# Staging S5 scan inputs in DRAM, running the scan ahead of three gate projections, and mid-chunk states on 128 lanes

## The chip, the cores and the metric

The kernel runs on one core of a Trainium2 chip. The metric is the device time of one execution in microseconds (us); the kernel before stands at a median of 2649.24 us over 3 runs (2646.02 to 2655.04). Engines are named as in the profile: PE is TensorE's matmul, PEld its weight load, DVE is VectorE, ACT is ScalarE, POOL is GpSimd, SP is SyncE, which issues most of the transfers.

## The reference

The kernel computes one step of a two-layer trunk for a prompt of 2048 positions and 8 samples of 4 positions, width 1024. Layer A is a chunked gMLP, which the change does not touch. Layer B is an S5 state-space mixer:

```python
xb, z = jnp.split(h @ w_in, 2, axis=-1)
xg = xb.astype(jnp.float32).reshape(bn, seq_len, N_GROUPS_B, SSM_GROUP)
bu_re = jnp.einsum('blgk,gpk->blgp', xg, bbr)
bu_im = jnp.einsum('blgk,gpk->blgp', xg, bbi)
acr, aci, hr, hi = lax.associative_scan(_combine, (ar, ai, bu_re, bu_im), axis=1)
y = jnp.einsum('gkp,blgp->blgk', cr, hr) - jnp.einsum('gkp,blgp->blgk', ci, hi)
y = y.reshape(bn, seq_len, EXP_B) + d_skip.astype(jnp.float32) * xb.astype(jnp.float32)
y = jax.nn.gelu(y).astype(h.dtype)
y = (y @ w_glu1 + b_glu1) * jax.nn.sigmoid(y @ w_glu2 + b_glu2)
out = (y * jax.nn.silu(z)) @ w_out
```

There are 64 groups of 16 channels, each with a complex state of 64 numbers. `xb` feeds the states; `z` is the gate, which is first needed in the gated unit after the states' output `y`.

## The kernel before, in words

The 2048 positions are cut into 128 chunks of 16, and each chunk into two halves of 8. `layer_b` runs in this order: the gate projection of position block 0 (`z_phase`, L817), the `xb` projections of blocks 0 and 1 (`xb_step`, L798), the gate projection of block 1, then the `xb` projections of blocks 2 and 3 mixed with eight calls of `state_in` (L838), the `scan` (L878), the gate projections of blocks 2 and 3, and the states' output `s5_out` (L889). `layer_c` (L966) then reads y back and runs the gated unit `glu` and the output projection.

A projection of a block is 8 weights of 24 PE matmuls (128x512) each: fp32 operands are split into two fp32r parts by ACT (`whi`, L68) and DVE (`wlo`, L69) and multiplied three times. Block 3, which also carries the samples, goes as halves of 256 and 288 columns, 48 matmuls per weight. In the profile these read `mm<-hn`. Each weight is a 512 KB load on SP's queue into `wst`, a pool of two buffers that is free again once DVE has made `wlo`. The gate z goes to DRAM (`zd`) from ACT's queue.

`state_in(u)` makes, for four groups per lane half (128 lanes), the chunk halves' state inputs: the first half's go to `G1` (L857), a tile of 128x2x32x128 fp32 (32 KB a partition) that stays in SBUF, the second half's to `S`. Sixteen DVE scalar_tensor_tensor of 128x128 (L862) add the decayed first half, and `advance` (L866) with steps 1, 2 and 4 combines chunks into spans of 8 chunks. `scan` runs over the 16 spans, serially, on DVE.

`s5_out` runs 16 units u, two (gh = 0, 1: the two lane halves) for each group set of four groups. For a pair of units there are

- loads on SP: T, Xo (two), Co for each unit,
- once a pair (gh = 0): `advance` down the tree with steps 4, 2, 1 (12 DVE tensor_tensor), and on POOL two times `gt` (L911) and `G` (L912), 128x512 each, which turn G1 into (first half's input + imaginary part of the decayed state),
- for each unit: ACT copies the chunk-start states into H (L917, 64x512), and eight DVE scalar_tensor_tensor of 64x128 (L919) write the mid-chunk states into H's second part,
- for each unit: four pairs of fp32 matmuls with 264 columns, `aux<-Xo,T` and `aux<-H,Co` (each shows as two records), the GELU on ACT (L927, `Y`), and stores of Y to DRAM (`yd`, `ysd`) on SP.

Which engine runs what when is set by the framework's scheduler from priorities. `p0` (L783) notes the priority before the last gate projection, and `s5_out`, written after it, is placed at that priority: its instructions and the gate projections written after `p0` are interleaved, s5_out first where it is ready. Before the change only block 3's gate projection stands behind `p0`. `load_y` (L987) reads y back (`yst<-yd`), ACT and DVE split it (L68, L69), and `mm<-y` is the first work of layer C.

Of the kernel before, what the change touches and what calls it, by code (L numbers as in the profile page):

```python
# [8 lines left out]
F32 = mybir.dt.float32  # L9
# [5 lines left out]
MUL, ADD, SUB = ALU.mult, ALU.add, ALU.subtract  # L15
# [3 lines left out]
NB = 4  # L19
# [3 lines left out]
AL = 512  # L23
TXP = 640
L = 16
NC_ = 128
G = 64
K16 = 16
CW = NC_ + 8
# [5 lines left out]
class Trunk:  # L35
# [701 lines left out]
    def layer_b(self, s0):  # L737
        with ExitStack() as sr:
            zp = s0.enter_context(self.pool("zp", 2))
            with ExitStack() as s1:  # L740
                hb3 = s1.enter_context(self.pool("hb3"))
                with ExitStack() as s2:
                    hb2 = s2.enter_context(self.pool("hb2"))
                    with ExitStack() as s3:
                        hb1 = s3.enter_context(self.pool("hb1"))
                        hbs = {1: hb1, 2: hb2, 3: hb3}
                        c2 = s3.enter_context(self.pool("c2"))
                        xf = s3.enter_context(self.pool("xf"))
                        self.xp = s3.enter_context(self.pool("xp2", 4))
                        g1 = self.load_gpre(c2, 1)  # L750
                        gens = [self.prep_block(b, self.x1c(b), self.x1s, g1, hbs[b], f"hb{b}")
                                for b in range(1, NB)]
                        self.hn1 += [next(g) for g in gens]
                        steps = (x for g in gens for x in g)
                        for fb in range(8):
                            self.z_phase(zp, [0], [fb])
                            if fb < 3:
                                next(steps)
                        for fb in range(8):
# [5 lines left out]
                    self.nc.vector.memset(S[:, :, :, 0], 0.0)  # L765
                    G1 = sr.enter_context(self.pool("gp", side="right")).tile([128, 2, 32, NC_], F32, name="G1")
                    with ExitStack() as s3:
                        xf = s3.enter_context(self.pool("xf2"))
                        sp = s3.enter_context(self.pool("sp", 2))
                        for i in range(4):  # L770
                            for gh in range(2):
                                self.xb_step(xf, i + 4 * gh, [2, 3])
                                if i:
                                    self.state_in(sp, S, G1, 2 * (i - 1) + gh)
                        for gh in range(2):
                            self.state_in(sp, S, G1, 6 + gh)
                        t1 = sp.tile([128, 2, 2, 4, 64], F32, tag="adv", name="sc", bufs=1)[:, :, :, 0, 0:32]
                        self.scan(S, t1)
                    opa = sr.enter_context(self.pool("opa", 3, side="right"))
                    self.z_phase(zp, [2])  # L780
                opb = sr.enter_context(self.pool("opb", 2, side="right"))
                fp = sr.enter_context(self.pool("fp", side="right"))
                p0 = self.tc.cur_priority  # L783
                self.z_phase(zp, [3])
            self.yq = s0.enter_context(self.pool("yq"))
            self.yp = s0.enter_context(self.pool("yp", 2))
            with self.tc.high_priority(offset=self.tc.cur_priority - p0):
                self.s5_out(fp, opa, opb, S, G1)
            self.y0 = self.load_y(0)

    def relay(self, dst, o, c0, n):
# [43 lines left out]
        for h in range(2):  # L835
            self.nc.sync.dma_start(X[:, :, h], s[h][:, g0:g0 + ng, :])

    def state_in(self, sp, S, G1, u):  # L838
# [19 lines left out]
        for g in range(gl, gl + 4):  # L858
            for r in range(2):
                for i in range(2):  # L860
                    x = S[:, r, g, 1:1 + NC_]
# [27 lines left out]
    def s5_out(self, fp, opa, opb, S, G1):  # L889
        nc, I = self.nc, self.I  # L890
        stt = nc.vector.scalar_tensor_tensor
        h0 = fp.tile([128, 64, 8], F32, name="h0")
        nc.sync.dma_start(h0, I["h0k"])
        for u in range(16):
            gl, gh, gu = (u // 2) * 4, u % 2, ((u // 2) % 2) * 4
            fb = u // 4 + 4 * gh
# [31 lines left out]
            d = self.yd[fb].rearrange("(h j) k g c -> h (j k) g c", h=2)  # L928
# [166 lines left out]
    def build(self):  # L1095
        tc = self.tc
        with self.ctx as s:
# [9 lines left out]
            t = lambda n, shape: dr.tile(shape, F32, name=n)  # L1107
# [4 lines left out]
            self.bind = [t(f"bind{i}", [128, 8, 128]) for i in range(8)]  # L1112
            self.xd = [t(f"xd{i}", [16, 16, 8, CW]) for i in range(8)]
            self.zd = [t(f"zd{i}", [128, NB, 16, 32]) for i in range(8)]
            self.zsd = [t(f"zsd{i}", [128, NS]) for i in range(8)]
            self.yd = [t(f"yd{i}", [16, 16, 8, NC_]) for i in range(8)]
            self.ysd = [t(f"ysd{i}", [4, 16, 8, 8]) for i in range(8)]
# [97 lines left out]
```

## Time and profile before

| | us |
|---|---|
| median of 3 runs | 2649.24 |
| the profiled execution's own time | 2648.36 |
| its span, first to last instruction | 2646.6 |
| PE busy over the span | 2577.8 (97%) |
| DVE, ACT, POOL busy | 1519.2 (57%), 906.4 (34%), 470.8 (18%) |
| s5_out's stretch, first `aux<-Xo,T` to last `aux<-H,Co` | about 1963.4 to 2088.4 |

All times are of one profiled execution; 1.8 us of its time lie outside the span. PE is close to fully busy over the whole program, so what is to be read are the stretches in which it is not. PE records of matmuls in a row overlap, so a mean duration is more than the distance from one to the next; the prices of matmuls are taken from unbroken chains of them. The granted clock column (PEclk) is 1.00 when TensorE is granted 2.4 GHz and 0.50 when it is granted 1.2 GHz.

### The profile page before, as it was taken

Reading aid. Unit: us, or ns where it says so; the run is one execution under the profiler, and the core shown is the slowest. Engines: PE = TensorE matmul, PEld = TensorE weight load, DVE = VectorE, ACT = ScalarE, POOL = GpSimd, SP = SyncE. Lnnn points to the kernel's source line nnn. Section 1 sums busy time; section 2 is a strip of 40 time slices with the busy share of each in tenths; the row PEclk is TensorE's granted clock in tenths of the full one; section 3 lists DMA queues with packets and bytes.
Section 4 is the critical chain, followed back from the end, with each engine's and each line's share of the span. In section 5 each row is a group of like instructions: output and inputs, shape, how many; then the busy total and the mean of one; then the engine's idle time right before and its main releaser. Section 6 shows DMA issues by size and latency. Waiting matters only on the chain.

```text
span 2646.6 us, 34651 instructions
## 1 busy us (share of the span) xinstructions
PE 2577.8 (97%) x13163; PEld 2192.5 (83%) x13163; DVE 1519.2 (57%) x2805; ACT 906.4 (34%) x1488; POOL 470.8 (18%) x644
## 2 busy tenths in 40 slices
PE   9999999999999999999999999999997899999998
PEld 7888877888878888887999877889986688888896
DVE  5974577743575633563733448314899746464645
ACT  3333343322333222432322334324644433333331
POOL 1454475100120000000000120000013212121220
PEclk9999999999999999999999999999998999999999
DMA  4253345422575222242322336445668735454542
GB/s 160 90 165 110 115 119 176 138 88 91 156 207 193 93 88 95 90 153 92 118 80 80 104 106 208 108 137 157 197 218 242 213 119 168 150 170 149 165 129 100
DMA packets 234839, 366.66 MB, mean 139 GB/s; under 512 B 64512, under 2 KB 154880, under 8 KB 234672
## 3 DMA queue, kind: packets, MB, share of 16 engines
q1 hardware_dynamic: 181344, 307.17, 36.7%
q0 software_dynamic: 13344, 36.63, 4.6%
q10 hardware_dynamic: 39984, 20.65, 2.9%
q8 instruction: 103, 1.69, 0.3%
q14 instruction: 64, 0.52, 0.1%
HBM read 307.45 MB, written 56.92 MB: 138 GB/s over the span
## 4 chain that ended last, share of the span: by engine, by line
PE 81%; DVE 10%; DMA 4%; issue 3%; POOL 1%; ACT 1%; SPq 1%; DVEq 0%; POOLq 0%; ACTq 0%
PE mm L59 79%; DVE wlo L69 1%; PE aux L59 1%; DVE H L919 1%; PE aux L137 1%; DVE adv L874 1%; DVE S L876 1%; DMA td<-vt 1%; DVE adv L873 1%; DMA x<-x1d 0%; DMA x<-in_xp_dram 0%; DVE adv L875 0%; POOL co L687 0%; DMA bind<-bo 0%; POOL ct L687 0%
## 5 line engine op out<-in xcount | busy, mean ns | idle before, releaser
L59 PE MATMUL mm<-hn,whi 128*128 128x512 f32 (+2 forms) x3840 | 1016.6, 353 | 3.4 <-ACT a L334 3.4
L69 DVE TENSOR_TENSOR wlo<-wst,whi 128x1024 fp32r<-128x1024 f32 x396 | 504.7, 1275 | 551.8 <-ACT whi L68 540.5
L59 PEld LDWEIGHTS mm<-hn,whi 128*128 128x128 f32 x3840 | 674.5, 189 | 92.1 <-ACT a L334 3.6
L68 ACT CAST whi<-wst 128x1024 fp32r<-128x1024 f32 x400 | 419.5, 1049 | 939.0 <-PE mm L59 811.3
L59 PE MATMUL mm<-hn,wlo 128*128 128x512 f32 (+2 forms) x1920 | 676.0, 352 | 3.7 <-DVE wlo L69 3.7
L59 PEld LDWEIGHTS mm<-hn,wlo 128*128 128x128 f32 x1920 | 362.7, 189 | 50.3 <-DVE wlo L69 4.5
L59 PE MATMUL mm<-whi,gs 128*128 128x512 f32 x1024 | 334.5, 399 | 10.6 <-ACT gs L68 5.1
L59 PE MATMUL mm<-y,whi 128*128 128x512 f32 (+2 forms) x1280 | 336.1, 351 | 3.4 <-ACT y L68 3.0
L59 PE MATMUL mm<-whi,hn 128*128 128x512 f32 x1024 | 325.7, 394 | 0.5 <-ACT hn L68 0.5
L59 PEld LDWEIGHTS mm<-y,whi 128*128 128x128 f32 x1280 | 224.2, 188 | 37.9 <-ACT y L68 3.8
L59 PEld LDWEIGHTS mm<-whi,gs 128*128 128x128 f32 x1024 | 194.6, 191 | 56.3 <-ACT gs L68 7.6
L59 PEld LDWEIGHTS mm<-whi,hn 128*128 128x128 f32 x1024 | 193.3, 189 | 43.8 <-ACT hn L68 0.7
L59 PE MATMUL mm<-y,wlo 128*128 128x512 f32 (+2 forms) x640 | 224.4, 351 | 0.0
L59 PE MATMUL mm<-wlo,hn 128*128 128x512 f32 x512 | 201.5, 393 | 3.6 <-DVE wlo L69 3.5
L59 PE MATMUL mm<-wlo,gs 128*128 128x512 f32 x512 | 202.2, 395 | 0.0
L59 PE MATMUL mm<-whi,m 128*128 128x512 f32 x512 | 159.8, 390 | 0.0
L69 DVE TENSOR_TENSOR gs<-gq,gs 128x512 fp32r<-128x512 f32 (+1 forms) x128 | 92.5, 723 | 108.9 <-ACT gs L68 108.6
L348 DVE SCALAR_TENSOR_TENSOR gq<-mm,lng,Rp 128x512 f32<-128x512 f32 x64 | 48.0, 750 | 173.2 <-PE mm L59 173.2
L68 ACT CAST gs<-gq 128x512 fp32r<-128x512 f32 (+1 forms) x128 | 80.2, 628 | 177.8 <-PE mm L59 168.7
L59 PEld LDWEIGHTS mm<-y,wlo 128*128 128x128 f32 x640 | 120.3, 188 | 16.2
L59 PEld LDWEIGHTS mm<-wlo,hn 128*128 128x128 f32 x512 | 96.9, 189 | 25.7 <-DVE wlo L69 4.6
L59 PEld LDWEIGHTS mm<-wlo,gs 128*128 128x128 f32 x512 | 97.5, 190 | 19.9
(291 smaller groups left out, 2684.8 us busy)
## 6 DMA issues: line engine op xcount, KB each, us to landing
wst<-in_wuz_dram SPq DMA_DIRECT2D x128, 512.0 KB, 3.4
wst<-in_wv_dram SPq DMA_DIRECT2D x64, 512.0 KB, 3.5
wst<-in_woa_dram SPq DMA_DIRECT2D x64, 512.0 KB, 3.3
wst<-in_wg_dram SPq DMA_DIRECT2D x64, 512.0 KB, 3.6
wst<-in_wib_dram SPq DMA_DIRECT2D x48, 512.0 KB, 4.2
wst<-in_wob_dram SPq DMA_DIRECT2D x32, 512.0 KB, 3.6
Xi<-xd SPq DMA_DIRECT2D x32, 272.0 KB, 4.2
Xo<-xd SPq DMA_DIRECT2D x32, 272.0 KB, 5.4
```

Of the source, the lines that this page charges most:

```text
L59: self.nc.tensor.matmul(out, lhsT, rhs, start=start, stop=stop)
L68: self.nc.scalar.copy(hi, src)
L69: (e or self.nc.vector).tensor_tensor(lo, src, hi.bitcast(F32), SUB)
L137: nc.tensor.transpose(b[:, k * 128:k * 128 + P], x[:, o:o + 128], self.ident[:P, :P])
L348: nc.vector.scalar_tensor_tensor(g3, s3, self.lng[:, db:db + 1], R, MUL, ADD)
L873: v.tensor_tensor(t[:, 0], d[0], S[:, :, g, src], MUL)
L874: v.tensor_tensor(t[:, 1], d[1], S[:, ::-1, g, src], MUL)
L876: v.tensor_tensor(S[:, :, g, dst], t[:, 0], S[:, :, g, dst], ADD)
L919: stt(H[q, g, CW:], S[p, r, gl + g, 0:NC_], self.d8[p, 0, r, gl + g:gl + g + 1], G1[p, r, gl + g], MUL, ADD)
```

## The change

- The gate projection of block 1 moves from ahead of the `xb` projections of blocks 2 and 3 to behind the scan, and `p0` is taken before it. So the gate projections of blocks 1, 2 and 3 all stand at the priority that lets `s5_out` interleave with them.
- `G1` is gone. `state_in(u)` fills a small tile `G` (128x2x4x128) and stores it to a DRAM tensor `gd[u]` (512 KB, ACT's queue). `s5_out` loads it back once a pair (`Go`, 512 KB, SP's queue, two buffers).
- POOL's 32 tensor_tensor (`gt`, `G`) and the 128 DVE scalar_tensor_tensor of 64x128 are replaced by 128 DVE scalar_tensor_tensor of 128x128 on `Go` (16 a pair, real and imaginary part), and 32 ACT copies of 64x512 put the result into H.
- The pool `opa` has 2 buffers by default in place of 3; T and Xo keep their own 4, so this meets Co (3 to 2) and the new Go.

```diff
@@ layer_b
-                        for fb in range(8):
-                            self.xb_step(xf, fb, [0, 1])
-                            if fb % 2 == 0:
-                                next(steps, None)
                         self.z_phase(zp, [1])
-                    S = self.hnp.tile([128, 32, 2, CW + 1], F32, tag="hn", name="S", align_bytes=AL).rearrange("p g r c -> p r g c")
-                    G1 = sr.enter_context(self.pool("gp", side="right")).tile([128, 2, 32, NC_], F32, name="G1")
...
+                            for fb in range(8):
+                                self.xb_step(xf, fb, [0, 1])
+                                if fb % 2 == 0:
+                                    next(steps, None)
+                            for _ in steps:
+                                pass
...
+                            for gh in range(2):
+                                self.state_in(sp, S, 6 + gh)
+                            t1 = sp.tile([128, 2, 2, 4, 64], F32, tag="adv", name="sc", bufs=1)[:, :, :, 0, 0:32]
+                            self.scan(S, t1)
+                        p0 = self.tc.cur_priority
                         self.z_phase(zp, [1])
-                    opa = sr.enter_context(self.pool("opa", 3, side="right"))
+                    opb = sr.enter_context(self.pool("opb", 2, side="right"))
+                    opa = sr.enter_context(self.pool("opa", 2, side="right"))
+                    fp = sr.enter_context(self.pool("fp", side="right"))
                     self.z_phase(zp, [2])
-                opb = sr.enter_context(self.pool("opb", 2, side="right"))
-                fp = sr.enter_context(self.pool("fp", side="right"))
-                p0 = self.tc.cur_priority
                 self.z_phase(zp, [3])
@@ state_in
+        G = sp.tile([128, 2, 4, NC_], F32, tag="G", name="G")
...
-                        nc.scalar.copy(S[p, r, g, 1:1 + CW] if h else G1[p, r, g], o[r * 64:r * 64 + 64])
+                        nc.scalar.copy(S[p, r, g, 1:1 + CW] if h else G[p, r, 2 * e:2 * e + 2], o[r * 64:r * 64 + 64])
+        nc.scalar.dma_start(self.gd[u], G)
...
-                    nc.vector.scalar_tensor_tensor(x, G1[:, r ^ i, g], self.d8[:, i, r, g:g + 1], x, MUL, ADD)
+                    x = S[:, r, gl + g, 1:1 + NC_]
+                    nc.vector.scalar_tensor_tensor(x, G[:, r ^ i, g], self.d8[:, i, r, gl + g:gl + g + 1], x, MUL, ADD)
@@ s5_out
             if gh == 0:
+                G = opa.tile([128, 2, 4, NC_], F32, tag="G", name="Go")
+                nc.sync.dma_start(G, self.gd[u // 2])
                 for i in (4, 2, 1):
                     self.advance(opb, S, gl, i, slice(0, NC_, 2 * i), slice(i, NC_, 2 * i))
-                gs = slice(gl, gl + 4)
-                for r in range(2):
-                    t = opb.tile([128, 4, NC_], F32, tag="gt", name="gt", bufs=1)
-                    d = self.d8[:, 1, r, gs].rearrange("p (g o) -> p g o", o=1).to_broadcast([128, 4, NC_])
-                    nc.gpsimd.tensor_tensor(t, d, S[:, 1 - r, gs, 0:NC_], MUL)
-                    nc.gpsimd.tensor_tensor(G1[:, r, gs], G1[:, r, gs], t, ADD)
+                for g in range(4):
+                    for r in range(2):
+                        for i in range(2):
+                            stt(G[:, r, g], S[:, r ^ i, gl + g, 0:NC_], self.d8[:, i, r, gl + g:gl + g + 1],
+                                G[:, r, g], MUL, ADD)
...
-                for g in range(4):
-                    stt(H[q, g, CW:], S[p, r, gl + g, 0:NC_], self.d8[p, 0, r, gl + g:gl + g + 1], G1[p, r, gl + g],
-                        MUL, ADD)
+                nc.scalar.copy(H[q, :, CW:], G[p, r])
```

The order that the scheduler makes of it shows at three places. The first is PE's order at the end of s5_out, up to the first matmul of layer C. Before the change (`mm<-y` is layer C):

```order
L59 MATMUL aux<-Xo,T 128x264 x3
L59 MATMUL aux<-H,Co 128x264
L59 MATMUL aux<-Xo,T 128x264
L59 MATMUL aux<-H,Co 128x264 x3
L59 MATMUL aux<-Xo,T 128x264 x2
L59 MATMUL aux<-H,Co 128x264
L59 MATMUL aux<-Xo,T 128x264 x2
L59 MATMUL aux<-H,Co 128x264 x3
L953 MATMUL aux<-ident,hp 64x128
L960 MATMUL aux<-ident,hs 128x128 x4
L59 MATMUL mm<-y,whi 128x512 x2
```

and with it:

```order
L59 MATMUL aux<-Xo,T 128x264
L59 MATMUL aux<-H,Co 128x264
L59 MATMUL mm<-hn,whi 128x288 x2
L59 MATMUL mm<-hn,wlo 128x288
L59 MATMUL mm<-hn,whi 128x256 x2
L59 MATMUL mm<-hn,wlo 128x256
L59 MATMUL mm<-hn,whi 128x288 x2
L59 MATMUL mm<-hn,wlo 128x288
L957 MATMUL aux<-ident,hp 64x128
L59 MATMUL mm<-hn,whi 128x256
L964 MATMUL aux<-ident,hs 128x128 x4
L59 MATMUL mm<-hn,whi 128x256
```

Before, the last units of s5_out stand back to back and layer C follows at once; the 253 halves of block 3's gate that the order has behind the first `aux<-Xo,T` are spread over the units before. Now 116 matmuls of 512 columns and 211 halves stand between the first `aux<-Xo,T` and the last `aux<-H,Co`, and 173 halves more between that and the first `mm<-y`. Ahead of the first `state_in` matmul, 192 matmuls of 512 columns (block 1's gate) are gone; between the last one and the first `aux<-Xo,T` stand 182 of 512 columns, where there were 108 of them and 131 halves.

The second place is DVE's order over one pair of units in the middle of s5_out. Before:

```order
L873 TENSOR_TENSOR adv<-d_72,S 128x8x16
L874 TENSOR_TENSOR adv<-d_72,S 128x8x16
L875 TENSOR_TENSOR adv<-adv 128x8x16
L876 TENSOR_TENSOR S<-adv,S 128x2x4x16
L873 TENSOR_TENSOR adv<-d_71,S 128x8x32
L874 TENSOR_TENSOR adv<-d_71,S 128x8x32
L875 TENSOR_TENSOR adv<-adv 128x8x32
L919 SCALAR_TENSOR_TENSOR H<-S,d_69,G_14456 64x128 x4
L876 TENSOR_TENSOR S<-adv,S 128x2x4x32
L873 TENSOR_TENSOR adv<-d_70,S 128x512
L874 TENSOR_TENSOR adv<-d_70,S 128x512
L919 SCALAR_TENSOR_TENSOR H<-S,d_69,G_14456 64x128 x4
```

and with the change:

```order
L878 TENSOR_TENSOR adv<-d_71,S 128x8x32
L879 TENSOR_TENSOR adv<-d_71,S 128x8x32
L880 TENSOR_TENSOR adv<-adv 128x8x32
L881 TENSOR_TENSOR S<-adv,S 128x2x4x32
L878 TENSOR_TENSOR adv<-d_70,S 128x512
L879 TENSOR_TENSOR adv<-d_70,S 128x512
L880 TENSOR_TENSOR adv<-adv 128x512
L881 TENSOR_TENSOR S<-adv,S 128x2x4x64
L917 SCALAR_TENSOR_TENSOR Go<-S,d_69,Go 128x128 x9
L878 TENSOR_TENSOR adv<-d_72,S 128x8x16
L917 SCALAR_TENSOR_TENSOR Go<-S,d_69,Go 128x128
L879 TENSOR_TENSOR adv<-d_72,S 128x8x16
```

The count for a pair is the same, 12 tensor_tensor and 16 scalar_tensor_tensor; the latter now write `Go`, which must have been loaded, where they wrote H from G1.

The third place is SP's queue in the middle of s5_out, with the change:

```order
L839 DMA Xo<-xd_102 128x4x136 x2
L81 DMA wst<-in_wib_dram 128x1024
L911 DMA Go<-gd_119 128x1024
L908 DMA Co<-cod_77 128x512
L934 DMA yd_133<-Y 128x4x128 x2
L935 DMA ysd_141<-Y 64x4x8
L81 DMA wst<-in_wib_dram 128x1024 x2
L904 DMA T<-td_90 128x512
L908 DMA Co<-cod_81 128x512
```

Here the loads of the gate's weights (`wst`) and of `Go` stand between the loads and stores of the units; before, the stretch had two weight loads of the gate, six of layer C, and no `Go`.

## Rows read from the trace of the kernel before

**Rows 1.** Windows: us, busy PE, PEld, DVE, ACT, POOL, PEclk, DMA share, GB/s.

```profile
1963.40:2088.40 125.00, 102.31 (x513) 88.37 (x514) 122.05 (x231) 58.35 (x126) 46.53 (x47) 0.89 0.85 250
2088.40:2098.40 10.00, 6.61 (x29) 4.58 (x27) 2.75 (x6) 4.51 (x8) 3.91 (x4) 1.00 0.95 271
```

**Rows 2.** PE's waits from 1815 to 2100: waiter and releaser, total, times, longest.

```profile
PE aux L59 <- DVE H L919: 14.8, 6, 4.0
PE aux L59 <- POOL gt L911: 5.5, 1, 5.5
PE mm L59 <- ACT y L68: 3.0, 2, 2.0
...
PE aux L59 <- DMA Xo<-xd: 1.5, 1, 1.5
PE mm L59 <- DVE y L69: 0.4, 1, 0.4
```

**Rows 3.** PE's groups by line in 1963.4 to 2088.4.

```profile
L59 PE MATMUL aux<-H,Co 128*128 128x264 f32 x128 | 44.4, 455 | 22.7 <-DVE H L919 14.8 <-POOL gt L911 5.5 <-issue 2.3
L59 PE MATMUL mm<-hn,whi 128*128 128x256 f32 (+1 forms) x168 | 40.6, 329 | 0.0
L59 PE MATMUL aux<-Xo,T 128*128 128x264 f32 x128 | 40.0, 407 | 1.5 <-DMA Xo<-xd 1.5
L59 PE MATMUL mm<-hn,wlo 128*128 128x288 f32 x85 | 28.4, 334 | 0.0
```

**Rows 4.** The chain from 1640 to 1960: start us, us, what.

```profile
1703.83 21.78 PE mm L59 x96
1726.21 89.02 PE mm L59 x456
```

**Rows 5.** PE's timeline at the end of s5_out: start us, us, what.

```profile
2085.66 1.05 PE L59 MATMUL aux<-Xo,T 128*128 128x264 f32 x4
2086.55 1.50 PE L59 MATMUL aux<-H,Co 128*128 128x264 f32 x6
```

**Rows 6.** DVE's groups by line in 1963.4 to 2088.4.

```profile
L919 DVE SCALAR_TENSOR_TENSOR H<-S,d,G 64x128 f32<-64x128 f32 x128 | 40.4, 375 | 0.7
L874 DVE TENSOR_TENSOR adv<-d,S 128x128 f32<-128x128 f32 (+2 forms) x21 | 22.5, 1074 | 0.0
```

**Rows 7.** DVE's groups by line in 1815 to 1935, where `state_in` runs.

```profile
L862 DVE SCALAR_TENSOR_TENSOR S<-G,d,S 128x128 f32<-128x128 f32 x128 | 35.0, 355 | 21.6 <-ACT S L857 21.6
...
L69 DVE TENSOR_TENSOR wlo<-wst,whi 128x1024 fp32r<-128x1024 f32 x11 | 13.4, 1222 | 10.5 <-ACT whi L68 10.4
L874 DVE TENSOR_TENSOR adv<-d,S 128x512 f32<-128x512 f32 (+2 forms) x23 | 13.3, 578 | 0.0
```

**Rows 8.** Windows, DVE alone: us, busy (instructions), PEclk, DMA share, GB/s.

```profile
1815.00:1935.00 120.00, 94.95 (x231) 1.00 0.61 185
```

**Rows 9.** Transfers in 1963.4 to 2088.4: total, and issues with median landing.

```profile
DMA packets 45764, 31.31 MB, mean 250 GB/s; under 512 B 6567, under 2 KB 40172, under 8 KB 45755
...
wst<-in_wg_dram SPq DMA_DIRECT2D x6, 512.0 KB, 3.7
zd<-z ACTq DMA_DIRECT2D x6, 256.0 KB, 4.7
yst<-yd SPq DMA_DIRECT2D x6, 256.0 KB, 4.9
wst<-in_wib_dram SPq DMA_DIRECT2D x2, 512.0 KB, 5.1
```

**Rows 10.** Windows of 10 us whose DMA share is over 1.

```profile
1960.00:1970.00 10.00, 8.49 (x62) 8.02 (x61) 9.79 (x13) 4.31 (x8) 5.64 (x5) 1.00 1.06 335
1970.00:1980.00 10.00, 7.69 (x45) 6.81 (x44) 9.79 (x24) 3.98 (x8) 1.44 (x2) 1.00 1.07 340
...
2010.00:2020.00 10.00, 6.36 (x37) 5.55 (x35) 9.76 (x16) 4.20 (x9) 5.43 (x5) 0.96 1.08 322
...
2040.00:2050.00 10.00, 6.75 (x40) 5.90 (x38) 9.79 (x15) 5.50 (x12) 6.15 (x6) 0.99 1.09 325
...
2070.00:2080.00 10.00, 4.85 (x10) 3.37 (x11) 9.82 (x19) 3.11 (x7) 4.98 (x5) 0.69 1.08 301
```

**Rows 11.** SP's waits in 1963.4 to 2098.4.

```profile
SPq L81 <- DVE wlo L69: 23.8, 5, 6.4
```

**Rows 12.** ACT's groups by line in 1963.4 to 2088.4.

```profile
L917 ACT COPY H<-S 64x512 f32<-64x512 f32 x32 | 19.9, 620 | 16.1 <-DVE S L876 10.0 <-DVE adv L874 5.7
```

More of the change, by code (lines that the diff above doesn't have):

```diff
@@ L745, in layer_b @@
                         hb1 = s3.enter_context(self.pool("hb1"))
[L746 to L752, printed above, removed]
@@ L753, in layer_b @@
-                        self.hn1 += [next(g) for g in gens]
-                        steps = (x for g in gens for x in g)
-                        for fb in range(8):
[L756 to L759, printed above, removed]
-                            self.xb_step(xf, fb, [0, 1])
-                            if fb % 2 == 0:
-                                next(steps, None)
@@ L763, in layer_b @@
-                        self.z_phase(zp, [1])
-                    S = self.hnp.tile([128, 32, 2, CW + 1], F32, tag="hn", name="S", align_bytes=AL).rearrange("p g r c -> p r g c")
-                    self.nc.vector.memset(S[:, :, :, 0], 0.0)
-                    G1 = sr.enter_context(self.pool("gp", side="right")).tile([128, 2, 32, NC_], F32, name="G1")
[L767 to L778, printed above, removed]
@@ L779, in layer_b @@
-                    opa = sr.enter_context(self.pool("opa", 3, side="right"))
+                        with ExitStack() as s4:
+                            hbs = {1: hb1, 2: hb2, 3: hb3}
+                            c2 = s4.enter_context(self.pool("c2"))
+                            xf = s4.enter_context(self.pool("xf"))
+                            self.xp = s4.enter_context(self.pool("xp2", 4))
+                            g1 = self.load_gpre(c2, 1)
+                            gens = [self.prep_block(b, self.x1c(b), self.x1s, g1, hbs[b], f"hb{b}")
+                                    for b in range(1, NB)]
+                            self.hn1 += [next(g) for g in gens]
+                            steps = (x for g in gens for x in g)
+                            for fb in range(8):
+                                self.z_phase(zp, [0], [fb])
+                                if fb < 3:
+                                    next(steps)
+                            for fb in range(8):
+                                self.xb_step(xf, fb, [0, 1])
[3 more added lines that the diff above has]
+                                pass
@@ new lines, in layer_b @@
+                        S = self.hnp.tile([128, 32, 2, CW + 1], F32, tag="hn", name="S",
+                                          align_bytes=AL).rearrange("p g r c -> p r g c")
+                        self.nc.vector.memset(S[:, :, :, 0], 0.0)
+                        with ExitStack() as s4:
+                            xf = s4.enter_context(self.pool("xf2"))
+                            sp = s4.enter_context(self.pool("sp", 2))
+                            for i in range(4):
+                                for gh in range(2):
+                                    self.xb_step(xf, i + 4 * gh, [2, 3])
+                                    if i:
+                                        self.state_in(sp, S, 2 * (i - 1) + gh)
+                            for gh in range(2):
+                                self.state_in(sp, S, 6 + gh)
+                            t1 = sp.tile([128, 2, 2, 4, 64], F32, tag="adv", name="sc", bufs=1)[:, :, :, 0, 0:32]
+                            self.scan(S, t1)
@@ L787, in layer_b @@
             with self.tc.high_priority(offset=self.tc.cur_priority - p0):
-                self.s5_out(fp, opa, opb, S, G1)
+                self.s5_out(fp, opa, opb, S)
             self.y0 = self.load_y(0)
@@ L836, in load_x, with state_in @@
             self.nc.sync.dma_start(X[:, :, h], s[h][:, g0:g0 + ng, :])
-    def state_in(self, sp, S, G1, u):
+    def state_in(self, sp, S, u):
         nc = self.nc
+        G = sp.tile([128, 2, 4, NC_], F32, tag="G", name="G")
         gl, g0 = 4 * u, (u % 2) * 4
@@ L887, in scan, with s5_out @@
             v.tensor_tensor(S[:, :, :, c], t1, t2, ADD)
-    def s5_out(self, fp, opa, opb, S, G1):
+    def s5_out(self, fp, opa, opb, S):
         nc, I = self.nc, self.I
@@ L904, in s5_out @@
             if gh == 0:
+                G = opa.tile([128, 2, 4, NC_], F32, tag="G", name="Go")
+                nc.sync.dma_start(G, self.gd[u // 2])
                 for i in (4, 2, 1):
                     self.advance(opb, S, gl, i, slice(0, NC_, 2 * i), slice(i, NC_, 2 * i))
-                gs = slice(gl, gl + 4)
-                for r in range(2):
-                    t = opb.tile([128, 4, NC_], F32, tag="gt", name="gt", bufs=1)
-                    d = self.d8[:, 1, r, gs].rearrange("p (g o) -> p g o", o=1).to_broadcast([128, 4, NC_])
-                    nc.gpsimd.tensor_tensor(t, d, S[:, 1 - r, gs, 0:NC_], MUL)
-                    nc.gpsimd.tensor_tensor(G1[:, r, gs], G1[:, r, gs], t, ADD)
+                for g in range(4):
+                    for r in range(2):
+                        for i in range(2):
+                            stt(G[:, r, g], S[:, r ^ i, gl + g, 0:NC_], self.d8[:, i, r, gl + g:gl + g + 1],
+                                G[:, r, g], MUL, ADD)
             H = opb.tile([128, 4, CW + NC_], F32, tag="H", name="H")
@@ L1114, in build @@
             self.zd = [t(f"zd{i}", [128, NB, 16, 32]) for i in range(8)]
+            self.gd = [t(f"gd{i}", [128, 2, 4, NC_]) for i in range(8)]
             self.zsd = [t(f"zsd{i}", [128, NS]) for i in range(8)]
```

2 lines of the change are left out of this document (removed).

## The prediction

> **What bounds the kernel now.** The page's first part comes first: PE is busy 97% of the span, so a change to work beside PE gains nothing unless it removes a stretch in which PE stands or runs slowly. The windows by stage show the only long one near this change, s5_out and the ten microseconds behind it [rows 1]: PE is busy 102.31 of 125.00 us at a mean granted clock of 0.89 of 2.4 GHz, then 6.61 of 10.00. DVE is busy 122.05 of the 125.00, so DVE sets the pace there. The waits say the same [rows 2]: PE stands on DVE's H (14.8 us) and once on POOL's gt (5.5), then on the first y (3.0 and 0.4). The list starts at 1815 and has no wait of PE before the 1.5 us ahead of the first Xo,T: state_in and the scan are covered by gate projections.
>
> How much can be won? I price PE's work at full clock. A 512-column matmul is 21.78/96 = 0.2269 us [rows 4]. The chain of 456 is 312 of these and 144 halves by the program's order: (89.02 - 70.8)/144 = 0.1266 for a half. Four records of 264 columns lie between the starts 2085.66 and 2086.55 [rows 5], 0.2225 each. The stage has 256 such records and 253 halves [rows 3]: 57.0 + 32.0, with 0.6 for transposes 89.6 of 125 us. The next 10 us hold 25 matmuls of layer C (29 records less 4 transposes), 5.7 us. So 95.3 of 135 us are work and **39.7 us are lost**: 22.7 + 3.4 us of standing [rows 1], and the remaining 13.6 us at the lower clock, 1.2 GHz, which agrees with 0.11 x 125 from the clock column.
>
> **The change, part by part.** *The move.* Behind the first Xo,T there are now 116 matmuls of 512 columns and 211 + 173 halves in place of 253 halves: 26.3 + 131 x 0.1266 = 42.9 us more work. It is missing ahead of it, so the first Xo,T comes at 1963.4 - 42.9 = 1920.5, if the stretch before stays unbroken. The scan's cover is as long as before: 182 x 0.2269 = 41.3 us against 108 x 0.2269 + 131 x 0.1266 = 41.1. The 1.5 us ahead of the first Xo,T stays in both. Let S be the new time from first Xo,T to the end of s5_out. Behind it come 173 halves (21.9 us), a wait for y, and the 25 matmuls (5.7). Layer C's first chain now has 21.9 us of cover; that could hide all 3.4 us of today's waits, or none, as y's eight tiles come one by one through two buffers. I keep the 3.4. The point that was 2098.4 is then 1920.5 + S + 21.9 + 3.4 + 5.7 = 1951.5 + S: **the gain is 146.9 - S**.
>
> *S by PE:* 57.0 + 26.3 + 211 x 0.1266 = 26.7 + 0.6 = 110.6 us. At the start the first pair needs, on DVE, 12 advances and 16 scalar_tensor_tensor at clean prices (below), 6.1 + 4.4, and two ACT copies, 1.2 [rows 12], 11.7 us, while PE has 1.8 + 33 x 0.2269 = 9.3 of work: 2.4 us of standing, so 113.0.
>
> *S by DVE.* Instructions are exchanged one for one (128 for 128), and a 64-lane one takes 375 ns where a 128-lane one takes 355 [rows 6, 7]: the lanes gain nothing. What goes is the slowing of the others: L874 takes 1074 ns on average beside POOL, 578 in state_in [rows 6, 7]. The window of state_in has the same count, 231 DVE instructions, in 94.95 us [rows 8] against 122.05 [rows 1]. Of it 35.0 are 128 of the 128x128 form, 0.273 apart, 13.4 eleven wlo, so 46.55/92 = 0.506 for an advance instruction. The new stage: 35.0 + 96 x 0.506 + wlo for 116/24 + 211/48 = 9.2 weights, 11.2 = 94.8, with the finals some 98. DVE no longer sets the pace, provided that POOL is what slowed it.
>
> The Trainium skill, page "SBUF — State Buffer", section "Who interferes with whom", says that a DVE instruction with two SBUF inputs contends with a GpSimd instruction that reads SBUF, and that DMA never contends with a compute engine. By that rule S stays at DVE's 98, under PE's 113, and rival B below is out. Its second half cannot be told from these rows, as the DMA share is 0.85 in the one window and 0.61 in the other.
>
> *S by the transfers.* Today 31.31 MB [rows 9]. New: six of the eight Go loads (two come ahead), 3.15 MB; 9.2 gate weights for today's 2 + 6 weights, 0.63; 9.2 stores of z for 6, 0.84; six y loads leave, -1.57: 34.4 MB. At the mean of the five slices whose engines are full, (335 + 340 + 322 + 325 + 301)/5 = 325 GB/s [rows 10], that is 106 us; at the stage's mean, 250, 137 us. The 250 comes with gaps in the queue: SP stands 23.8 us on wst buffers that DVE has not yet released [rows 11], with every later load behind. DVE has 24 us less to do, but there are nine such weights, and Go and Co share two buffers per kind. I take the middle rate, 287 GB/s: **S = 120**. It holds the 2.4 us of the start and 7 us of short stops; falls of the clock lie among these.
>
> *The rest costs nothing.* The 8 stores of gd lie in state_in, at a DMA share of 0.61 [rows 8] and with no PE wait; without that cover, each would have to be late by the whole scan to be felt. The 32 ACT copies are 32 x 0.620 = 19.8 us [rows 12] on an engine busy 58 of 125 [rows 1], and the two that now follow a pair's last DVE instruction lie behind the 14 to 18 halves (about 2 us) that PE's order puts between units; without these, 1.2 us a unit. POOL's work is off the path.
>
> Sum: 146.9 - 120 = 26.9 us. 2648.36 - 26.9 = 2621.5; the median of the runs is 0.9 higher, so **2622**.
>
> **The rivals.** *A, PE is the bound.* The transfers keep up: S = 113.0, gain 33.9, or 37.3 if y is in time: 2612 to 2615. For it: five slices already run at 325 GB/s, at which 34.4 MB fit. Against it: full slices now alternate with emptier ones.
>
> The Trainium skill's same page, section "Summary: rules for kernel authors", counts about 358 GB/s between HBM and SBUF; an estimate by that figure is 96 us for the 34.4 MB, which would make A the case. No full slice here reached it (340 at most).
>
> *B, DVE stays slow*, because the transfers and not POOL slow it: 122.05 + 2.2 wlo = 124.7 us, and with half of today's 13.6 us of low clock S = 131: gain 15.9, 2633. For it: the DMA share is higher in the slow window. Against it: the scalar_tensor_tensor is hardly slower there, 375 to 355.
>
> *C, PE's fixed order keeps its waits.* If H is still late for each pair, work that stands behind it in the order does not help: 110.6 + 14.8 + 5.5 + 13.6 = 144.5, gain 2.4, 2647, no difference that counts. Against it: the time that DVE needs for a pair falls below PE's.
>
> *D, slower: SP's queue.* A weight load waits 23.8/5 = 4.8 us for its buffer [rows 11]; T, Co and Go behind it come late, with two Co buffers in place of three. If PE feels it at all nine weights, that is 43 us, and with a lower clock behind each wait (today 13.6 us for seven waits, 1.9 each) 17 more: S = 113 + 60 = 173, gain -26, 2675. It is slower than before from S = 146.9 on, 3.8 us a weight. Against it: today eight such loads cost PE 1.5 us on a load in all [rows 2].
>
> **How the numbers follow.** The forecast (2615 to 2630) has 0.44, A 0.22, B 0.17, C 0.10, D 0.07. About 0.3%, 8 us, is what a measurement here can tell from no change: faster is forecast, A and B, 0.83; same is C, 0.10; slower D, 0.07. The range is that of the first three with the ends of their unknown costs: below, A with a stage that also loses its 2.4 us, 2609, and 3 us for the spread of the runs; above, B with the whole 13.6 us of low clock, 2640, and 3 us: 2606 to 2643.
>
> **What would show it.** First Xo,T near 1920; no wait on H in most pairs; DVE's advance near 0.55 us in place of 1.07; s5_out about 120 us at 280 GB/s or more, with PE's waits on Xo, Co or Go loads, or on wlo; 173 halves behind the last unit; layer C from about 2071. It would be wrong if advances stay near 1 us (B), if PE waits on Go in each pair (C), if SP's waits on wlo grow and PE's waits on loads with them (D), or if a wait appears ahead of the first Xo,T, where I assume none.

## The result

The changed kernel takes 2624.18 us (median of 4 runs, 2621.18 to 2624.96) where the kernel before takes 2648.03 on the same chip: a ratio of 0.9903, with a 95% interval of 0.9883 to 0.9923. On a second chip it was 0.9914 (0.9900 to 0.9929). The forecast was 2622, in a range of 2606 to 2643, faster with 0.83.

The profiled execution has a span of 2622.3 us, PE is busy 98% of it, POOL 437.8 us where it was 470.8. The windows by stage (busy PE, PEld, DVE, ACT, POOL, PEclk, DMA share, GB/s) are s5_out, the remaining gate, and the start of layer C; the first answers to [rows 1]:

```profile
1917.00:2039.50 122.50, 114.15 (x586) 98.55 (x585) 92.42 (x232) 77.25 (x158) 11.30 (x14) 0.97 0.99 306
2039.50:2064.90 25.40, 22.13 (x179) 21.90 (x177) 6.74 (x7) 9.99 (x22) 3.89 (x4) 1.00 0.62 193
```

DVE is busy 92 of 122 us, no longer 122 of 125. PE is the busiest engine, at a clock of 0.97 of 2.4 GHz. The transfers run at a share of 0.99. PE's waits from 1700 to 2110, which answer to [rows 2], are:

```profile
PE aux L59 <- ACT Y L931: 7.3, 4, 3.8
PE mm L59 <- ACT y L68: 3.6, 2, 3.3
PE aux L59 <- issue: 0.8, 1, 0.8
PE mm L59 <- DVE y L69: 0.2, 1, 0.2
PE aux L59 <- DMA Co<-cod: 0.2, 1, 0.2
```

No wait on H and none on POOL is left. The waits now name ACT: its `Y` frees the PSUM bank that the next `aux<-Xo,T` writes. PE's timeline (start, us, what, the wait before it) shows the two longest, and the ends of the stretch:

```profile
1916.99 1.94 PE L59 MATMUL aux<-Xo,T 128*128 128x264 f32 x8
...
1981.31 1.16 PE L59 MATMUL aux<-Xo,T 128*128 128x264 f32 x4 [2.51 <-ACT Y L931]
1998.42 1.25 PE L59 MATMUL aux<-Xo,T 128*128 128x264 f32 x2 [3.80 <-ACT Y L931]
...
2039.16 0.27 PE L957 MATMUL aux<-ident,hp 128*64 128x128 f32 x1
...
2064.89 2.50 PE L59 MATMUL mm<-y,whi 128*128 128x512 f32 x5 [3.27 <-ACT y L68]
```

s5_out takes 2039.16 - 1916.99 = 122.2 us, up to the first of its transposes. In the trace 201 halves of the gate lie ahead of the last `aux<-H,Co` (start 2037.78) and nine more ahead of the first transpose; the 211 given with the order run to the last transpose. DVE's groups in it, which answer to [rows 6], have the advance at 564 ns in place of 1074:

```profile
L917 DVE SCALAR_TENSOR_TENSOR Go<-S,d,Go 128x128 f32<-128x128 f32 x128 | 35.3, 344 | 2.3 <-DMA Go<-gd 2.2
...
L879 DVE TENSOR_TENSOR adv<-d,S 128x128 f32<-128x128 f32 (+2 forms) x21 | 11.8, 564 | 0.0
```

The transfers of the stretch, which answer to [rows 9]:

```profile
DMA packets 46279, 37.48 MB, mean 306 GB/s; under 512 B 6892, under 2 KB 38667, under 8 KB 46269
...
wst<-in_wib_dram SPq DMA_DIRECT2D x10, 512.0 KB, 6.2
Go<-gd SPq DMA_DIRECT2D x7, 512.0 KB, 5.3
...
zd<-z ACTq DMA_DIRECT2D x10, 256.0 KB, 4.9
```

Why was ACT late at 1998? The chain of what PE waited for (start, us, what) passes through a DMA issue on ACT:

```profile
1991.39 6.08 DMA yd<-Y
...
1997.55 0.39 ACTq L834
...
1997.98 0.40 ACT Y L931
...
1998.42 1.25 PE aux L59 x2
```

and ACT's timeline at that place:

```profile
1990.67 0.69 ACT L931 ACTIVATE Y<-aux 128x264 f32<-128x264 f32 x2
1997.55 0.39 ACTq L834 DMA_DIRECT2D zd<-z  x1
1997.98 0.39 ACT L931 ACTIVATE Y<-aux 128x264 f32<-128x264 f32 x1 [6.62 <-DMA yd<-Y]
```

ACT had done two of this unit's four Y by 1991 and then stood 6.62 us. Its next row is the issue of a gate store, `zd<-z` (L834), and that one had waited for the landing of `yd<-Y`, a store of SP's. In the program, such an issue waits on one of the eight completion counts that SP's and ACT's transfers use in turn:

```
L834 DMA zd_109<-z 128x512 [waits DMAHW0_49,Activation_49]
```

So a store that nobody needs soon held the GELU that PE needed, on the same in-order engine. The same pattern, with the load of Co in front, stands before the stop of 2.51 us. The experiments test whether these stops, the bytes, or DVE set the stage.

### The profile page after: what moved, and what is told of

It reads as the page before. It is cut to its first block, busy times and chain, and to the rows that moved or that the text cites. A ratio compares the mean times of both kernels' runs of the same rounds, so it can differ in the third digit from the quotient of the medians.

```text
span 2622.3 us, 34670 instructions
## 1 busy us (share of the span) xinstructions
PE 2566.8 (98%) x13163; PEld 2184.5 (83%) x13163; DVE 1489.2 (57%) x2805; ACT 923.0 (35%) x1520; POOL 437.8 (17%) x612
## 4 chain that ended last, share of the span: by engine, by line
PE 82%; DVE 7%; DMA 5%; issue 2%; POOL 2%; ACT 1%; SPq 0%; ACTq 0%; DVEq 0%; POOLq 0%
PE mm L59 79%; PE aux L59 3%; DVE wlo L69 1%; PE aux L137 1%; DMA bind<-bo 1%; DMA wst<-in_wib_dram 1%; DMA yst<-yd 1%; DMA x<-x1d 0%; DMA Go<-gd 0%; DMA Co<-cod 0%; DMA td<-vt 0%; DMA x<-in_xp_dram 0%; POOL co L687 0%; ACT whi L68 0%; POOL ct L687 0%
## 5 line engine op out<-in xcount | busy, mean ns | idle before, releaser
L68 ACT CAST whi<-wst 128x1024 fp32r<-128x1024 f32 x400 | 419.6, 1049 | 915.5 <-PE mm L59 769.6
L68 ACT CAST gs<-gq 128x512 fp32r<-128x512 f32 (+1 forms) x128 | 80.2, 628 | 177.0 <-PE mm L59 168.1
L59 PEld LDWEIGHTS mm<-whi,m 128*128 128x128 f32 x512 | 96.1, 188 | 20.6
```

Source lines behind the costliest of these rows:

```text
L59: self.nc.tensor.matmul(out, lhsT, rhs, start=start, stop=stop)
L68: self.nc.scalar.copy(hi, src)
```

## The experiments

Ratios are to the kernel before on the same chip, with their 95% intervals.

| run | median us | ratio (interval) |
|---|---|---|
| changed kernel, first chip | 2624.18 | 0.9903 (0.9883 to 0.9923) |
| changed kernel again, e10_after_again | 2625.82 | 0.9914 (0.9900 to 0.9929) |
| e1_pool_kept | 2642.16 | 0.9976 (0.9966 to 0.9986) |
| e2_no_move | 2632.78 | 0.9942 (0.9926 to 0.9959) |
| e3_dve_in_sbuf | 2629.66 | 0.9930 (0.9916 to 0.9945) |
| e4_go_twice | 2617.42 | 0.9877 (0.9858 to 0.9896) |
| e5_zd_pool | 2617.92 | 0.9894 (0.9874 to 0.9914) |
| e6_more_bytes | 2623.96 | 0.9907 (0.9889 to 0.9925) |
| e7_pool_idle_work | 2635.34 | 0.9948 (0.9931 to 0.9965) |
| e8_zd_pool_z3_early | 2608.90 | 0.9854 (0.9834 to 0.9874) |
| e9_sbuf_zd_pool | 2628.58 | 0.9920 (0.9903 to 0.9937) |
| e11_z3_early | 2609.75 | 0.9860 (0.9844 to 0.9877) |

### The parts of the change: e1, e2, e3

**e1_pool_kept** takes the changed kernel and makes the mid-chunk states as before:

```diff
-                            stt(G[:, r, g], S[:, r ^ i, gl + g, 0:NC_], self.d8[:, i, r, gl + g:gl + g + 1],
-                                G[:, r, g], MUL, ADD)
+                    nc.gpsimd.tensor_tensor(t, d, S[:, 1 - r, gs, 0:NC_], MUL)
+                    nc.gpsimd.tensor_tensor(G[:, r], G[:, r], t, ADD)
...
-                nc.scalar.copy(H[q, :, CW:], G[p, r])
+                    stt(H[q, g, CW:], S[p, r, gl + g, 0:NC_], self.d8[p, 0, r, gl + g:gl + g + 1], G[p, r, g],
+                        MUL, ADD)
```

> The changed order and the DRAM staging stay, but the mid-chunk states are made as before: two gt and two G tensor_tensor on POOL per pair, and 64-lane scalar_tensor_tensor into H on DVE (gt takes its 2 KB from the tile of the finals). Theory: POOL beside DVE slows DVE's advances to about 1 us each again, DVE needs about 125 us for the stage and sets S; time about 2633 (2629 to 2640), the L879 group near 1.0 us. Rival 1, the transfers set S anyway at about 122 us: time as the changed kernel, 2624, with advances at 1.0 us. Rival 2, it is the transfers that slow DVE: the advances stay at about 0.57 us although POOL works.

Measured 0.9976, 2642.16: order and DRAM alone give a quarter of the gain, less than expected. A DVE group over the stage (1912 to 2051.2) and the first of PE's waits:

```profile
L879 DVE TENSOR_TENSOR adv<-d,S 128x128 f32<-128x128 f32 (+2 forms) x21 | 17.3, 822 | 0.0
```

```profile
PE aux L59 <- DVE H L926: 9.5, 5, 3.2
```

The advance is at 0.82 us where the changed kernel has 0.56, and PE waits on H again. Both rivals fall.

**e2_no_move** puts block 1's gate and `p0` back, and keeps the rest:

```diff
-                        p0 = self.tc.cur_priority
-                        self.z_phase(zp, [1])
...
                     self.z_phase(zp, [2])
+                p0 = self.tc.cur_priority
                 self.z_phase(zp, [3])
```

> DRAM staging and DVE-alone states stay; the gate projection of block 1 goes back ahead of the xb projections of blocks 2 and 3, and p0 goes back behind block 2's gate. Theory: PE has 89.6 us of work in the stage, DVE about 97, the transfers about 34.5 MB, 113 us at the 306 GB/s that the changed kernel reached, so s5_out takes about 113 us in place of 125 and the wait for y at its end stays at 3 to 4 us: about 2636 (2631 to 2640). Rival: the order is what made the whole gain, and without it PE waits on H as before: 2647.

Measured 0.9942, 2632.78. s5_out takes 111.5 us of the expected 113:

```profile
1962.30:2073.80 111.50, 95.85 (x529) 84.27 (x528) 95.02 (x238) 74.01 (x159) 8.91 (x14) 0.95 1.03 319
```

PE has 91.6 us of work in it, not 89.6, as 269 halves of the gate stand in it where the kernel before has 253, and PE stands 14.8 us behind ACT's Y. Against this run the move of block 1's gate is worth 7 to 10 us: from 0.9942 to 0.9903 the intervals lie apart, to the second measurement's 0.9914 they overlap.

**e3_dve_in_sbuf** is the kernel before with one edit: DVE makes the states in place in G1, POOL has no part, and there is neither DRAM nor move.

```diff
-                    nc.gpsimd.tensor_tensor(t, d, S[:, 1 - r, gs, 0:NC_], MUL)
-                    nc.gpsimd.tensor_tensor(G1[:, r, gs], G1[:, r, gs], t, ADD)
+                            stt(G1[:, r, g], S[:, r ^ i, g, 0:NC_], self.d8[:, i, r, g:g + 1], G1[:, r, g], MUL, ADD)
...
+                nc.scalar.copy(H[q, :, CW:], G1[p, r, gl:gl + 4])
```

> The kernel before with one edit: POOL's gt and G and the 64-lane instructions are replaced by 16 scalar_tensor_tensor of 128x128 a pair on DVE, in place in G1, and ACT copies; G1 stays in SBUF and the order stays. Theory: advances fall to about 0.57 us, DVE needs about 97 us, the transfers (31.3 MB at 306 GB/s) 102 us: s5_out takes 102 to 108 us, time about 2629 (2625 to 2635). Rival: DVE's slowness came from the transfers, advances stay at about 1 us, time 2648.

Measured 0.9930, 2629.66, as the theory had it. The stage, about 104 us long, and its advance:

```profile
1960.00:2065.00 105.00, 94.99 (x516) 82.28 (x515) 91.04 (x230) 75.11 (x160) 9.83 (x15) 0.97 1.00 299
```

```profile
L874 DVE TENSOR_TENSOR adv<-d,S 128x128 f32<-128x128 f32 (+2 forms) x21 | 11.9, 566 | 0.0
```

This edit, which takes POOL out, is worth 16 us by itself (2646.08 to 2629.66), most of the whole change. The DRAM staging without the move (e2 against e3) costs something between nothing and a few us; the intervals overlap. Staging and move together add to e3 what lies between 0.9930 and 0.9903 or 0.9914, 4 to 7 us, again with intervals that overlap.

### What slows DVE: e7

```diff
+                q7 = fp.tile([128, 512], F32, tag="f", name="q7").rearrange("p (g c) -> p g c", g=4)
+                for r in range(2):
+                    nc.gpsimd.tensor_tensor(q7, d, S[:, 1 - r, gl:gl + 4, 0:NC_], MUL)
+                    nc.gpsimd.tensor_tensor(q7, q7, d, ADD)
```

> The changed kernel with idle work on POOL: per pair four tensor_tensor of 128x512 into a tile that nobody reads, two of them reading S, as many as the kernel before had; no byte is moved more. Theory: they slow DVE's advances and scalar_tensor_tensor by about 25 us over the stage (advance groups from 0.57 to about 1 us), DVE needs about 123 us and again sets the pace of the first pairs: 2630 to 2642. Rival: what slowed DVE in the kernel before was something else: 2624, advances at 0.57 us.

Measured 0.9948, 2635.34. The stage and two DVE groups in it:

```profile
1919.80:2052.80 133.00, 118.70 (x589) 101.62 (x588) 117.86 (x231) 77.28 (x158) 47.48 (x47) 0.95 0.93 284
```

```profile
L917 DVE SCALAR_TENSOR_TENSOR Go<-S,d,Go 128x128 f32<-128x128 f32 x128 | 59.6, 531 | 1.4 <-POOL q L922 1.2
L879 DVE TENSOR_TENSOR adv<-d,S 128x128 f32<-128x128 f32 (+2 forms) x21 | 12.7, 604 | 0.0
```

DVE's busy time rises from 92.4 to 117.9 us, the 25 expected, but not where it was expected: the idle work now runs beside the scalar_tensor_tensor, and it is these that go from 344 to 531 ns, while the advances stay near 0.6 us. Five of them take 4.68 us while four of POOL's idle operations run, from 1952.29 to 1956.98:

```profile
1952.45 4.68 DVE L917 SCALAR_TENSOR_TENSOR Go<-S,d,Go 128x128 f32<-128x128 f32 x5
```

PE's waits name ACT's Y here (12.8 us), but ACT's copies ahead of Y stand up to 6.1 us on DVE's `Go`: through ACT, DVE sets the pace again. It is POOL, then, and which DVE instruction pays depends on what runs beside it. How it pays shows in the timelines of the kernel before, POOL's and DVE's:

```profile
1994.72 1.19 POOL L911 TENSOR_TENSOR gt<-d,S 128x512 f32<-128x512 f32 x1 [10.08 <-DVE S L876]
```

```profile
1994.61 0.39 DVE L873 TENSOR_TENSOR adv<-d,S 128x128 f32<-128x128 f32 x1
1994.92 1.26 DVE L874 TENSOR_TENSOR adv<-d,S 128x128 f32<-128x128 f32 x1
1996.21 0.29 DVE L875 TENSOR_TENSOR adv<-adv 128x128 f32<-128x128 f32 x1
```

L873 and L874 are the same size. L874, begun beside POOL's gt, ends at 1996.18: that is gt's end, 1995.91, and about the 0.3 us between one such instruction and the next. It stood still while POOL worked. By the Trainium skill, page "SBUF — State Buffer", section "Who interferes with whom", a DVE instruction with two SBUF inputs contends with a GpSimd instruction that reads SBUF, and DMA contends with no engine; for DVE the runs agree with both halves, the first by these rows, the second by the advance at 564 ns under a DMA share of 0.99 beside 578 under 0.61 [rows 7, 8].

### Bytes or ACT's queue: e4, e6, e5

**e4_go_twice** leaves out six of eight Go loads:

```diff
-                G = opa.tile([128, 2, 4, NC_], F32, tag="G", name="Go")
-                nc.sync.dma_start(G, self.gd[u // 2])
+                G = Gs[(u // 2) % 2]
```

> The changed kernel without six of its eight Go loads: two Go tiles are loaded once and used in turn, so the mid-chunk states of six pairs start from other groups' inputs; every instruction on DVE, ACT and PE stays. 3.15 MB less cross in s5_out. Theory 1, bytes set S (37.48 MB at 306 GB/s, 122 us): S falls by 10 us to its PE bound of 113, time about 2615. Theory 2, ACT's queue sets it (issues of zd in front of Y that wait for another transfer's completion count): S falls by little, 2 to 4 us, time 2620 to 2624.

Measured 0.9877, 2617.42, nearly what the bytes would give. By itself that cannot tell bytes from queues, since fewer transfers also hold fewer completion counts; PE's stops behind ACT's Y fell to 0.6 us. The scheduler's order changed too: 102 matmuls of 512 columns and 120 halves stand among the units, where there were 116 and 201.

**e6_more_bytes** adds transfers that nobody waits for:

```diff
+            nc.sync.dma_start(self.yx[fb].rearrange("(h j) k g c -> h (j k) g c", h=2)[0][:, gu:gu + 4], Y[:, :, 0:NC_])
```

> The changed kernel with one more store of Y's first half per unit into a DRAM tensor that nobody reads: 16 more stores of 256 KB on SP's queue, 4.19 MB. Theory 1, bytes set S: 4.19 MB at 306 GB/s are 13.7 us, time about 2638. Theory 2, bytes count only where they delay an issue: the transfers ran at 325 GB/s in the run with zd on POOL, so 41.7 MB fit in 128 us; time 2628 to 2634. If the transfers have room, 2624 to 2626.

Measured 0.9907, 2623.96: no change against the changed kernel. In 125 us from the same start it moved

```profile
DMA packets 50517, 40.68 MB, mean 325 GB/s; under 512 B 6492, under 2 KB 42627, under 8 KB 50507
```

This is 2.4 MB more than the changed kernel moved in the same 125 us (38.28), at a rate 6% higher. So the changed kernel's 306 GB/s was not a ceiling, though its DMA share read 0.99. Whether the bytes cost the stage something, this run does not show: the scheduler put 310 halves of the gate among e6's units, where there were 201, and its s5_out ends at 2055. That work can cover what the bytes took, so only the whole times are compared.

**e5_zd_pool** moves the two gate stores off ACT's queue:

```diff
-                        nc.scalar.dma_start(self.zsd[fb], zs)
-                nc.scalar.dma_start(self.zd[fb][:, b], z)
+                        nc.gpsimd.dma_start(self.zsd[fb], zs)
+                nc.gpsimd.dma_start(self.zd[fb][:, b], z)
```

> The changed kernel, with the stores of the gate z (zd and zsd) issued from POOL's queue in place of ACT's, so that no issue in ACT's order waits for a completion count that SP's transfers hold. In the changed kernel PE's stops of 2.51 and 3.80 us stand behind ACT's Y, and ACT stands behind such an issue. Theory 1, the transfers set S (0.99 DMA share): the stops are only the place where the lack of bytes shows, time 2624 within 2 us. Theory 2, the stops are ACT's own queue: they go, with the lower clock behind them, time about 2614 to 2618.

Measured 0.9894, 2617.92. The time's interval overlaps that of the changed kernel; its trace is clear. Stage and waits:

```profile
1917.10:2035.00 117.90, 115.58 (x622) 101.39 (x621) 91.97 (x233) 79.30 (x161) 15.12 (x30) 1.00 1.03 325
```

```profile
PE mm L59 <- ACT y L68: 4.0, 2, 3.7
PE aux L59 <- DMA Co<-cod: 2.2, 2, 1.8
```

No stop behind ACT's Y is left, the clock does not fall, and s5_out ends 114 us after its start (2031 against 1917), near PE's own 110.6 us. From 1917 to 2031 it moved

```profile
DMA packets 45045, 37.31 MB, mean 327 GB/s; under 512 B 6366, under 2 KB 38176, under 8 KB 45034
```

That is what the changed kernel moved in its 122.5 us (37.48 MB), so the bytes had not set those 122 us. Theory 2 holds for the stops.

### The wait for y, and the fastest version: e8, e11, e9

The first y cast comes last in ACT's order, behind the copies of block 3's gate. ACT's timeline in the changed kernel (start, us, what):

```profile
2061.70 1.04 ACT L68 CAST whi<-wst 128x1024 fp32r<-128x1024 f32 x1 [4.05 <-DMA wst<-in_wg_dram]
...
2064.12 0.20 ACT L832 COPY zs<-mm 128x32 f32<-128x32 f32 x1
2064.20 0.64 ACT L68 CAST y<-yst 128x512 fp32r<-128x512 f32 x1
```

The first two y tiles had been issued at 1980. By the code, y also lacks a place until then: pool `yq` is opened where block 3's input has been freed, and that input is read to the end of the last gate. But PE's wait of 3.27 us begins at 2061.62, with the end of the gate's last matmul, and the y cast begins only at 2064.20: these 2.6 us are ACT's order, two casts of weights (`whi`, L68) and the last copies of z. The place alone would have let y go at 2061.6.

**e8_zd_pool_z3_early** is e5 with block 3's gate ahead of block 2's:

```diff
-                    self.z_phase(zp, [2])
-                self.z_phase(zp, [3])
+                    yp0 = sr.enter_context(self.pool("yp0", side="right"))
+                    self.z_phase(zp, [3])
+                    self.z_phase(zp, [2])
```

> zd and zsd stores on POOL, and block 3's gate ahead of block 2's: the y tile lies where block 3's input lay, so its first cast waits for the last matmul of block 3's gate. The y loads get one buffer of their own for the first call (T goes from 4 buffers to 3 for the space). Theory: the wait of 3.3 to 3.7 us for y and the lower clock behind it (about 3 us) go: 4 to 7 us less than with zd on POOL alone, about 2612. Rival: y is late because its last tiles are stored late, and the order of the gates does not count: 2618, the wait stays.

**e11_z3_early** is the same edit with the stores left on ACT:

> Block 3's gate ahead of block 2's, own buffer for the first y loads, T from 4 buffers to 3, but zd and zsd stay on ACT's queue. Theory: the two losses are independent, so this one gives the wait for y (3.3 us) and the lower clock behind it, 5 to 7 us: 2617 to 2620; PE's stops behind ACT's Y stay at 6 to 8 us. Rival: what the y wait costs is taken by the stops in s5_out: 2623.

Measured 0.9854 (2608.90) and 0.9860 (2609.75), the same within their intervals, and the fastest of all. PE's waits in e8 from 1880 to 2200, and below them those of e11 to 2110, complete:

```profile
PE aux L59 <- DMA Xo<-xd: 1.7, 1, 1.7
PE aux L59 <- DMA Co<-cod: 0.4, 1, 0.4
```

```profile
PE aux L59 <- ACT Y L934: 2.9, 1, 2.9
PE aux L59 <- issue: 1.7, 1, 1.7
```

The wait for y is gone in both. The expectation of two independent losses was wrong: with block 3's gate first, most of ACT's stops went too, without touching its queue, so moving the stores gains nothing measurable on top. Block 3's gate has two stores per weight and half-size matmuls, and the order puts 251 (e8) and 269 (e11) halves among the units, where there were 201. Why the stops went was not separated further, nor was the place of `y` from its rank in ACT's order in these two runs.

**e9_sbuf_zd_pool** adds the stores on POOL to e3 (the same two lines as e5):

> The kernel before with DVE-alone mid-chunk states in G1 (as e3_dve_in_sbuf, no DRAM, no move) and the zd and zsd stores on POOL's queue. Its stage has 89.6 us of PE work against 97 of DVE. Theory: DVE now sets the stage (about 98 to 100 us, from 103 in e3_dve_in_sbuf), so the move of block 1's gate is worth the rest: time 2624 to 2627, and 6 to 8 us stay that only fill can cover. Rival: the move and the DRAM are worth nothing once ACT's queue is free: 2618, as with zd on POOL in the changed kernel.

Measured 0.9920, 2628.58: no gain over e3. There ACT's Y waits mostly for something else, the sample's stores from its own buffers:

```profile
ACT Y L923 <- DMA ysd<-Y: 11.4, 5, 4.3
```

The theory's 98 to 100 us for the stage was missed. The rival falls too: it gives 2618, and without the move the time was 2628.58.

**e10_after_again** repeats the changed kernel.

> The changed kernel once more, unedited, on the chip that runs the other two of this call, so that they can be compared: 2624 beside about 2648 for the kernel before.

It gave 0.9914; its trace has the same waits (7.9 us behind ACT's Y, 3.7 for y).

## Why the prediction was right, and where it was not

**The prize of 39.7 us** was right. e8 removes every wait that the prediction counted, and at the same record of layer C (2600 from the last) it stands at 2079.3 us against 2120.6 in the kernel before, 41.3 earlier; 2.3 of these were there before the two orders part (about 1740), an ordinary difference of two executions. That leaves 39.0. Its split was not right: the 13.6 us put down to the lower clock agree with 0.11 x 125 by chance, since the clock column also counts time in which PE stands. The stretches at 1.2 GHz in the kernel before are these:

```profile
1988.42:1995.25 6.83, 5.18 (x15) 4.36 (x16) 6.67 (x15) 2.15 (x5) 0.53 (x1) 0.50 0.55 160
2019.14:2025.97 6.83, 5.64 (x15) 4.62 (x16) 6.65 (x18) 1.98 (x5) 0.95 (x1) 0.50 0.42 123
2049.86:2056.69 6.83, 5.98 (x17) 4.96 (x18) 6.69 (x17) 0.78 (x2) 1.29 (x1) 0.50 0.57 171
2073.75:2080.58 6.83, 5.43 (x12) 3.79 (x13) 6.62 (x16) 2.18 (x5) 2.34 (x2) 0.50 1.14 320
```

PE is busy in 22.2 of the 27.3 us, so the clock cost 11.1 us, and 2.5 of the 13.6 stay unassigned.

**The move.** First Xo,T was forecast at 1920.5 and came at 1917.0; 2.2 of these 3.5 us were there before the two orders part. No wait appeared ahead of it.

**DVE** was forecast at some 98 us with advances near 0.55 us; it was 92.4 with 0.564. Rival B is out, by e7 and e3.

**S = 120** was the step that failed, though its size came close (122.2) by luck. It was put down to the transfers: 34.4 MB at a middle rate of 287 GB/s. In fact 37.5 MB moved, since two yd stores, two y loads, one Go load and some gate loads and stores more fell into the stage than counted, and at 306 GB/s; two errors that cancel. And e5 shows that the bytes did not set the stage: 37.3 MB crossed in 114 us. The sum that fits is PE's: 110.6 us of work, 8.3 us of stops (7.3 + 0.8 + 0.2), and one fall of the clock, which began in the stop of 3.80 us:

```profile
1996.61:2003.44 6.83, 5.01 (x18) 4.60 (x19) 6.66 (x16) 3.06 (x6) 0.00 (x0) 0.50 1.08 317
2000.00:2010.00 10.00, 10.00 (x55) 9.27 (x55) 5.57 (x11) 7.00 (x15) 0.21 (x1) 0.83 1.09 369
```

At 1.2 GHz PE worked for 5.01 us (it stood for the rest of the first row), which cost 2.5 us; 110.6 + 8.3 + 2.5 = 121.4, and about 1 us of the 122.2 stays unassigned. The stops were rival A's missing piece: with the stores off ACT's queue (e5) the stage took 114 us, A's 113. The prediction costed the z stores as bytes only, and said of ACT that it had room, by its busy time (58 of 125 us [rows 1]). It did not ask what an issue in ACT's order waits for. The 2.4 us at the start were 0.8.

**The wait for y** was kept at 3.4 us and came to 3.3, but not for the loads of y that the text named, the first two of which had been issued 80 us ahead. The y cast stood behind block 3's gate, and 2.6 us of the wait are ACT's order; whether y's place in block 3's input would have held it too is argued from the code and not shown. Block 3's gate stood last before the change as well, but was done among the units; the move left its end behind them. A fall of the clock behind this wait, to 1.2 GHz from 2064.88 to 2068.29, was not in the sum:

```profile
2064.88:2068.29 3.41, 3.40 (x8) 2.76 (x9) 1.54 (x3) 0.47 (x1) 0.00 (x0) 0.50 0.88 258
```

It cost 1.7 us.

**The sum:** 26.9 us were forecast for the point that was at 2098.4, and the same matmul of layer C starts at 2072.6, 25.8 earlier: first Xo,T came 3.5 us sooner than forecast, S was 2.2 longer, and the stretch behind it took 33.4 us for 31.0, 1.7 of the difference by the clock. Later in layer C another 1.5 us went, which was not followed up: 2648.36 - 2624.06 = 24.3 between the two profiled executions, 23.9 between the medians.

**The rivals.** C (waits on H) is out: none is left. D (SP's queue) is out as a cost: PE waited 0.2 us on a load. The first half of D's mechanism, an issue that waits and holds what stands behind it, was there, on ACT and not on SP.

As to the Trainium skill's 358 GB/s between HBM and SBUF (page "SBUF — State Buffer", section "Summary: rules for kernel authors"), the row from 2000 to 2010 above moved 369 GB/s, so it is no ceiling for a stretch of 10 us here; e5 held 327 over its stage of 114 us.

## What to carry to other kernels

An engine's busy time says nothing about its issues: a DMA issue in the order of an engine that also feeds PE's buffers can hold it for the landing of another queue's transfer, so look for the rows between a late operation and the one before it. A DVE that is busy all the time may be slowed by POOL and not by its own work; compare the same instruction in a stretch where POOL is idle. A transfer share near 1 is no proof that bytes are the bound: take out a stop, and see whether the same bytes go in less time, as in e5.

## What had not been expected of the hardware

A DMA share of 0.99 still left room: the 37 MB that took the changed kernel's stage 122 us crossed in 114 once the stops were gone (e5, 327 GB/s where it had been 306), and in e6 the share read 1.05 (1917 to 2040). And POOL's work cost DVE about as much in scalar_tensor_tensor (344 to 531 ns, e7) as it had in the advances (564 to 1074 ns), so neither kind is safe beside it. That the former stood at 375 ns in the kernel before [rows 6] had looked like immunity; in its trace 122 of the 128 ran with no tensor_tensor of POOL beside them, at 347 ns in the mean, and the other six took 950.
